# Output projection of a gated block as four pairs of block products, with weight sums made in DRAM

## The chip, the cores and the metric

The kernel runs on one core of a Trainium2 chip. The metric is the device time of one execution in microseconds, as the median of several runs. The profile is of one execution and gives the span from its first to its last instruction.

## What is computed

A hybrid block on x of shape (1, 1024, 1024), all in float32. The input is normalised and projected; an attention branch and a pooling branch give 512 channels each; each is projected to 1024 channels, gated, and the sum goes through the output projection, the residual and a last norm:

```python
a = jnp.einsum('bsc,cd->bsd', y_attn, w_branch_attn)
p = jnp.einsum('bsc,cd->bsd', y_pool, w_branch_pool)
gate_a, gate_p = jnp.split(jax.nn.sigmoid(g_merge), 2, axis=-1)
merged = gate_a * a + gate_p * p
h = h + jnp.einsum('bsd,de->bse', merged, w_out)
return rms_norm(h, norm_final)
```

## The kernel before

Every float32 product is made of three matmuls of reduced float32 parts: an operand is split into a high part (a copy on ScalarE that rounds) and a low part (a subtraction on VectorE), and hi x hi, hi x lo and lo x hi are summed in PSUM. `split` (used by `operand`, `put` and `split_tile`) is that pair of instructions. A matmul has a stationary operand of 128x128 and a moving one of up to 512 columns.

The work runs in stages, on a list of items: the input projection of the latents; fourteen `Pair` items; the up-projections of the latents; attention over eight heads, in whose gaps the eight items of the pooling branch's projection (`run_branch_p`) run; eight `BranchItem`s for the attention branch; and the output projection.

A `Pair` computes two 128-channel rows of the input projection at once. It treats the 2x2 blocks of the weights (A11 to A22, each split in four tiles) and of the input (`B`, seven block combinations b11, b21, b22, t1 to t4 that are made once) by Winograd's variant of Strassen's scheme: seven block products of 12 matmuls in place of eight, with sums S1 to S4 of the A blocks made on VectorE (`both`) and additions out of PSUM afterwards. `load` fetches w_z, `preps` lists the steps that make the operands of the next item, and `tick` runs one of them after each product.

The pooling branch's gate is fetched in halves into `go` buffers, multiplied with the product in PSUM and stored in DRAM (`mp_d`). A `BranchItem` t loads w_ba, its gate, `mp_d[t]` and one row tile of w_o, multiplies, adds, and splits the merged tile and the w_o tile into high and low parts in SBUF. The output projection then takes eight row tiles of 128 tokens, each as two halves of 512 columns over eight blocks of channels (24 matmuls for a half); the last row tile is cut in 512, 256 and 256 columns to shorten its end. Each row adds the residual, is squared and summed on ScalarE, scaled on VectorE and stored.

The order of the instructions on each engine comes from `Plan.order`, a list scheduler: it gives each operation a cost, takes the one that can start first, and among those that start within 30 ns the one that comes first in the program. Buffers come from rings of tags (`SLOTS`): 45 "t" slots of 1024 floats per partition, two each of wh, wl and go, one wr, and eight PSUM banks (s two double ones, p two, o, f). A tag's slots are handed out strictly in the order in which the program first uses the buffers. All DMAs are issued in order on SP.

Of the kernel before, what the change touches and what calls it, by code (L numbers as in the profile page):

```python
# [14 lines left out]
P = 128  # L15
# [194 lines left out]
def hybrid_block_kernel(  # L210
# [42 lines left out]
    def dram(rows, name):  # L253
        b = Buf(lambda: tc.dram_tile([rows, T], F32, name=name), None)
        return View(b, 0, rows, 0, T)
# [116 lines left out]
    def dma(o, x):  # L372
        v = o if isinstance(o, View) else x
        p0, p1, c0, c1 = v.box
        plan.add(
            "SP",
            lambda: nc.sync.dma_start(real(o), real(x)),  # L377
            450,
            views(x),
            views(o),  # L380
            (p1 - p0) * (c1 - c0) * 4,
        )
# [86 lines left out]
    mp_d = [dram(P, f"mp_d{t}") for t in range(8)]  # L469
# [411 lines left out]
    merged = [None] * 8  # L881
    wo = [None] * 8


    class Pair(Item):
# [3 lines left out]
        ORDER = (("A11", "b11"), ("S2", "t2"), ("S1", "t1"), ("S3", "t3"), ("A12", "b21"), ("A22", "t4"), ("S4", "b22"))  # L889

        def __init__(self, i, posts, beside=()):
            self.i, self.posts, self.beside = i, posts, dict(beside)
            self.turn = len(items)
            self.src = w_z[i]
# [8 lines left out]
        def operand(self, name):  # L903
            j = len(self.ops)
            t = buf(("wh", "t", "wl", "t", "wh", "t", "wl")[j], T, F32R, "wp")
            split(t[:, lft], t[:, rgt], self.q[name])
# [7 lines left out]
        def preps(self):  # L914
# [4 lines left out]
                lambda: (self.both("S1", "A21", "A22", A, "A22"), self.both("S3", "A11", "A21", S, "A21")),  # L919
                lambda: (self.both("S2", "S1", "A11", S, "A11"), self.operand("S2")),  # L920
                lambda: self.operand("S1"),
                lambda: self.operand("S3"),
                lambda: self.operand("A12"),
                lambda: (self.both("S4", "A12", "S2", S, "A12"), self.operand("S4")),
            ]

        def product(self, bank, which, first):
# [4 lines left out]
            if which in self.beside:  # L932
                self.beside[which].go(self)
            a, b = self.ORDER[which]
            for k, ((ah, al), (bh, bl)) in enumerate(zip(self.ops[a], B[b])):
# [9 lines left out]
        def run(self, it, tick):  # L945
# [17 lines left out]
            self.product(c, 2, True)  # L963
            tt(c22, c, c21, ALU.add)
            tick()
            self.product(b, 3, False)
# [3 lines left out]
            self.product(a, 4, False)  # L970
            tt(c11, a, state["r"][:, lft], ALU.mult)
            tick()
            self.product(b, 5, False)
            tt(c21, b, c21, ALU.add)
            times(c21, lft)
            self.posts[1](o2)
            tick()
            self.product(c, 6, False)
            tt(c12, c, c12, ALU.add)
            times(c12, rgt)  # L980
            self.posts[0](o1)
            tick()
# [3 lines left out]
    def step_on(n):  # L986

        for _ in range(n):
# [3 lines left out]
            pair = isinstance(it, Pair)  # L992
# [4 lines left out]
            while ready[0] < min(i + 2, len(items)):  # L997
                nxt = items[ready[0]]
                ready[0] += 1
                todo += nxt.preps() if isinstance(nxt, Pair) else [nxt.split]  # L1000
# [66 lines left out]

    items.append(KrItem(w_kr, 32, 8, run_kr))
# [27 lines left out]
    gate_pair(14, [(4, q), (6, kv)])  # L1096
    for p in range(4):
# [11 lines left out]

    def run_branch_p(t):  # L1110
        def run(it):
            mov = halves(yp)
            for h, c in enumerate((lft, rgt)):
                g = buf("go", 512, F32, "go")
                dma(g, gate_d[8 + t][:, c])
# [9 lines left out]
                tt(g, ps, g, ALU.mult)  # L1125
                dma(mp_d[t][:, c], g)
# [8 lines left out]

    class BranchItem(Item):
        def __init__(self, t):
# [3 lines left out]
        def load(self):  # L1141
            super().load()
            self.g, self.m = t32("gate"), t32("mp")
            dma(self.g, gate_d[self.t])
            dma(self.m, mp_d[self.t])

        def go(self, it):
            t, g = self.t, self.g
            raw = t32("wo")
            dma(raw, w_o[t])  # L1150
            acc = next_acc()
            prod(acc, it.h, it.l, halves(ys))
            wo[t] = (tr("woh"), tr("wol"))
            for c in (lft, rgt):
                if c is lft or t < 4:
                    split(wo[t][0][:, c], wo[t][1][:, c], raw[:, c])
                else:
                    late.append((wo[t][0][:, c], wo[t][1][:, c], raw[:, c]))
            for ps, a, b in acc.spans:
                tt(g[:, a:b], ps, g[:, a:b], ALU.mult)  # L1160
            tt(g, g, self.m, ALU.add)
            merged[t] = split_tile(g)

    late = []
    raw_tag[0] = "t"
    for t in range(8):
        items.append(BranchItem(t))

# [90 lines left out]

    for v in late:  # L1260
        split(*v)
    nf = t32("nf")
    dma(nf, nfin)
    for i in range(8):
        sl = slice(128 * i, 128 * i + 128)
        res = t32("res")
        dma(res, xr[sl, :])
        last = i == 7
        cuts = [0, 512, 768, T] if last else [0, 512, T]
        tags = "pps" if last else "pp" if i % 2 else "of"  # L1270
        ss, st = cell(3), cell()
        junk = t32("junk")
        spans = list(zip(cuts, cuts[1:]))
        for n, (a, b) in enumerate(spans):
            c = slice(a, b)
# [104 lines left out]
```

## Time and profile before

| | us |
|---|---|
| median of 3 runs | 711.28 |
| lowest, highest | 710.94, 712.90 |
| profiled execution, device time | 712.28 |
| its span | 710.2 |
| TensorE busy | 691.1 |
| VectorE busy | 524.2 |
| ScalarE busy | 319.7 |
| GpSimd busy | 104.8 |

The busy time of TensorE counts overlapping matmuls once. The share of a whole span is an average over stages; what one stage costs is read from windows of that stage. Idle time of an engine that isn't the bottleneck costs nothing by itself.

### The profile page before, as it was taken

What the parts mean: (1) busy time and instruction counts of PE and PEld (TensorE: products, weight loads), DVE (VectorE), ACT (ScalarE), POOL (GpSimd) and SP (SyncE); (2) the same over time, 40 slices, a digit from 0 to 9 for tenths busy, and PEclk for the clock granted to TensorE, in tenths of its full rate; (3) what the DMA queues carried; (4) which work ended last, traced back from release to release, by engine and by line L of the source; (5) the groups of instructions that cost most, each with busy time, mean ns of one, the idle gap of its engine ahead of it and who ended that gap; (6) DMA issues with size and microseconds to landing.
All of it is one profiled execution on the core that took longest, in us unless ns stands there. A gap on an engine that the chain in (4) does not pass through costs nothing.

```text
span 710.2 us, 9562 instructions
## 1 busy us (share of the span) xinstructions
PE 691.1 (97%) x3428; PEld 581.1 (82%) x3428; DVE 524.2 (74%) x823; ACT 319.7 (45%) x587; POOL 104.8 (15%) x140
## 2 busy tenths in 40 slices
PE   8999999999999999999998999999999999999996
PEld 6878888888878878888786799989999777888885
DVE  5688898777978689789869678887887859932223
ACT  5864424331423344333346467666666525421112
POOL 0020100300002030300101044545443100000000
PEclk9999999999999999999999999999999999999999
DMA  8957433122715436233777986554322499413131
GB/s 313 375 177 260 149 119 120 68 111 99 279 59 179 177 118 235 91 132 103 284 256 293 325 187 189 142 138 109 106 75 74 160 326 409 143 60 118 60 118 60
DMA packets 39567, 120.70 MB, mean 170 GB/s; under 512 B 5088, under 2 KB 6240, under 8 KB 39520
## 3 DMA queue, kind: packets, MB, share of 16 engines
q1 hardware_dynamic: 39520, 120.09, 49.4%
q8 instruction: 27, 0.44, 0.2%
q14 instruction: 20, 0.16, 0.1%
HBM read 81.14 MB, written 37.88 MB: 168 GB/s over the span
## 4 chain that ended last, share of the span: by engine, by line
PE 83%; DMA 6%; DVE 5%; ACT 2%; issue 2%; SPq 1%; DVEq 0%; ACTq 0%
PE ps L275 28%; PE pb L275 22%; PE po L275 12%; PE sc L275 7%; PE o L275 5%; PE pf L275 5%; PE pt L282 4%; DMA wr<-w_bp 2%; DMA wr<-w_uq 1%; DMA wo<-w_o 1%; DVE lo L308 1%; SPq L377 1%; DMA x<-xT 1%; DMA wr<-w_uv 1%; DVE ra L308 1%
## 5 line engine op out<-in xcount | busy, mean ns | idle before, releaser
L275 PE MATMUL pb<-t,wp 128*128 128x512 f32 x504 | 121.6, 390 | 0.0
L275 PE MATMUL ps<-xa,wp 128*128 128x512 f32 x392 | 113.0, 390 | 0.0
L275 PEld LDWEIGHTS pb<-t,wp 128*128 128x128 f32 x504 | 94.5, 188 | 19.8 <-DVE z L308 0.2
L298 ACT CAST wp<-wr 128x512 fp32r<-128x512 f32 x98 | 58.9, 619 | 102.2 <-DVE wr L308 38.3
L275 PEld LDWEIGHTS ps<-xa,wp 128*128 128x128 f32 x392 | 73.6, 188 | 15.2
L308 DVE TENSOR_TENSOR wp<-wr,wp 128x512 fp32r<-128x512 f32 x98 | 72.6, 756 | 8.8 <-ACT wp L298 8.8
L322 POOL TENSOR_SCALAR pr<-pr,small 128x384 f32<-128x384 f32 (+4 forms) x64 | 48.3, 759 | 72.1 <-DVE small L348 56.6
L290 ACT ACTIVATE pr<-sc,small 128x384 f32<-128x384 f32 (+4 forms) x64 | 47.7, 746 | 20.6 <-DVE small L357 19.7
L308 DVE TENSOR_TENSOR pT<-pt,pT 128x512 fp32r<-128x512 f32 (+1 forms) x80 | 48.6, 633 | 8.9 <-ACT pT L298 8.3
L357 DVE TENSOR_REDUCE small<-sc 128x1 f32<-128x128 f32 (+3 forms) x64 | 47.5, 750 | 9.2 <-PE sc L275 8.7
L308 POOL TENSOR_TENSOR z<-z,sig 128x512 f32<-128x512 f32 x16 | 23.5, 1493 | 199.7 <-ACT sig L290 197.3
L275 PE MATMUL po<-woh,hi 128*128 128x512 f32 (+1 forms) x136 | 51.3, 377 | 0.0
L275 PE MATMUL po<-woh,lo 128*128 128x512 f32 (+1 forms) x136 | 51.3, 377 | 0.0
L275 PE MATMUL po<-wol,hi 128*128 128x512 f32 (+1 forms) x136 | 51.2, 377 | 0.0
L298 ACT CAST pT<-pt 128x512 fp32r<-128x512 f32 (+1 forms) x80 | 41.2, 545 | 17.2 <-PE pt L282 16.5
L275 PE MATMUL o<-pT,v 128*128 128x256 f32 (+1 forms) x320 | 47.7, 282 | 0.6 <-DVE oa L308 0.4
L275 PEld LDWEIGHTS o<-pT,v 128*128 128x128 f32 x320 | 43.7, 189 | 3.2 <-DVE oa L308 0.8
L308 DVE TENSOR_TENSOR z<-pb,z 128x512 f32<-128x512 f32 x42 | 28.9, 689 | 23.3 <-PE pb L275 18.3
L308 DVE TENSOR_TENSOR res<-po,res 128x512 f32<-128x512 f32 (+1 forms) x17 | 11.2, 660 | 46.9 <-PE po L275 46.9
L275 PE MATMUL ps<-xb,wp 128*128 128x512 f32 x112 | 43.6, 389 | 0.0
L282 PE MATMUL pt<-ident,pr 128*128 128x128 f32 x288 | 42.1, 274 | 0.0
L275 PE MATMUL ps<-t,wp 128*128 128x512 f32 x168 | 41.1, 391 | 0.8 <-DVE z L308 0.8
(192 smaller groups left out, 1382.8 us busy)
## 6 DMA issues: line engine op xcount, KB each, us to landing
wr<-w_z SPq DMA_DIRECT2D x30, 512.0 KB, 4.9
gate_d<-z SPq DMA_DIRECT2D x16, 512.0 KB, 2.6
xt<-xr SPq DMA_DIRECT2D x8, 512.0 KB, 10.3
go<-gate_d SPq DMA_DIRECT2D x16, 256.0 KB, 2.8
mp_d<-go SPq DMA_DIRECT2D x16, 256.0 KB, 2.8
gate<-gate_d SPq DMA_DIRECT2D x8, 512.0 KB, 7.3
mp<-mp_d SPq DMA_DIRECT2D x8, 512.0 KB, 8.2
wo<-w_o SPq DMA_DIRECT2D x8, 512.0 KB, 8.7
```

Source lines behind the costliest of these rows:

```text
L275: nc.tensor.matmul(real(o), real(a), real(b), start=s, stop=e, **kw)
L282: nc.tensor.transpose(real(o), real(a), real(ident))
L290: nc.scalar.activation(real(o), real(x), func, scale=real(scale), **kw)
L298: lambda: nc.scalar.copy(real(o), real(x)),
L308: plan.add(eng, lambda: e.tensor_tensor(real(o), real(a), real(b), op), c, [a, b], [o], port=port)
L322: e.tensor_scalar(real(o), real(a), real(s1), real(s2), op0, op1)
L357: lambda: nc.vector.tensor_reduce(real(o), real(a), axis=AX.X, op=ALU.max, negate=True),
L377: lambda: nc.sync.dma_start(real(o), real(x)),
```

## The change

The output projection becomes Strassen's scheme too. The merged tiles are stored in DRAM (`m_d`, two halves of 512 channels) and read back as blocks of 128 tokens; `Ahead` makes the first product (A11 b11) of four pairs of row tiles, and four `OutPair`s make the other six. The blocks of w_out and their four sums t1 to t4 are split as moving operands while the `BranchItem`s run. The sums are made in DRAM during the `Pair` stage: a plain transfer copies one block, and a transfer issued by GpSimd adds a second, negated on ScalarE where needed; hooks (`after`) tie each transfer to a product of some `Pair`. The products of the `Pair`s come in another order, with fewer additions on VectorE and more copies on ScalarE. The pooling branch's gated rows stay in SBUF (`mp`), loaded per head during attention, and the buffers `mp_d` are gone.

```diff
+    def dma_add(o, x):
+        plan.add(
+            "POOL",
+            lambda: nc.gpsimd.dma_start(real(o), real(x), accum_op=ALU.add),
+            1200,
+            views(o, x),
+            views(o),
...
-        ORDER = (("A11", "b11"), ("S2", "t2"), ("S1", "t1"), ("S3", "t3"), ("A12", "b21"), ("A22", "t4"), ("S4", "b22"))
+        ORDER = (("A11", "b11"), ("A12", "b21"), ("S2", "t2"), ("S1", "t1"), ("S3", "t3"), ("S4", "b22"), ("A22", "t4"))
...
-            self.product(a, 0, True)
-            acopy(c21, a)
+            b = buf("p", 512, F32, "pb")
+            self.product(b, 0, True)
+            acopy(c11, b)
             tick()
-            b = buf("p", 512, F32, "pb")
-            self.product(b, 1, True)
-            tt(c12, b, c21, ALU.add)
+            self.product(a, 1, True)
+            tt(c11, a, c11, ALU.add)
+            times(c11, lft)
...
+    def take(name, src, k):
+        def f(late):
+            rows = slice(128 * k, 128 * k + 128)
+            n = buf("go", 512, F32, "neg")
+            dma(n, src[rows, :], late)
+            act(n, n, AF.Copy, scale=-1.0)
+            dma_add(wt_d[name][rows, :], n)
+        return f
...
+    hooks = {1: [copy("t1", w_top, 512), copy("t3", w_low, 512)]}
+    for k, n in enumerate((2, 3, 4, 6)):
+        hooks[n] = [take("t1", w_top[:, 0:512], k), take("t3", w_top[:, 512:T], k)]
+    hooks[7] = [copy("t2", wt_d["t3"], 0)]
+    hooks[8] = [lambda late: dma_add(wt_d["t2"], w_top[:, 0:512])]
+    hooks[10] = [copy("t4", wt_d["t2"], 0)]
+    for k in range(4):
+        hooks.setdefault(11 + k // 2, []).append(take("t4", w_low[:, 0:512], k))
...
     def run_branch_p(t):
...
-                g = buf("go", 512, F32, "go")
-                dma(g, gate_d[8 + t][:, c])
...
-                tt(g, ps, g, ALU.mult)
-                dma(mp_d[t][:, c], g)
+                tt(g[:, c], ps, g[:, c], ALU.mult)
...
     class BranchItem(Item):
...
+            for n in BLOCKS[self.t : self.t + 1]:
+                src, c = blocks_at[n]
+                for j in range(2):
+                    raw = t32("wo")
...
+            for raw in self.blocks:
+                w = tr("wo")
+                split(w[:, lft], w[:, rgt], raw)
+                W.setdefault(BLOCKS[t], []).append((w[:, lft], w[:, rgt]))
+            for n, ps in enumerate(acc.halves):
+                c = (lft, rgt)[n]
+                tt(g[:, c], ps, g[:, c], ALU.mult)
+                tt(g[:, c], mp[t][:, c], g[:, c], ALU.add)
+                dma(rows_of(t)[:, c], g[:, c])
...
+    def rows_in(o, i, half):
+        dma(
+            o.via(lambda a: a.rearrange("p (k c) -> p k c", k=4)),
+            m_d[half][:, 128 * i : 128 * i + 128].via(lambda a: a.rearrange("(k p) c -> p k c", p=P)),
+        )
...
+    class Ahead:
...
+        def run(self, it, tick):
+            tick()
+            s1, s2 = buf("s", T, F32, "ps"), buf("s", T, F32, "ps")
+            first["b"] = [buf("o", 512, F32, "pb"), buf("f", 512, F32, "pb"), s1[:, lft], s2[:, lft]]
+            first["c"] = [s1[:, rgt], s2[:, rgt], None, None]
+            for i in range(4):
+                t, bank = self.ops[i], first["b"][i]
+                for k, (bh, bl) in enumerate(W["b11"]):
+                    ah, al = t[:, 128 * k : 128 * k + 128], t[:, 512 + 128 * k : 640 + 128 * k]
+                    mms([(bank, ah, bh, k == 0, False), (bank, ah, bl, False, False), (bank, al, bh, False, k == 3)])
+                tick()
...
+    class OutPair(Pair):
+        TAGS = ("t", "wh", "wl", "t", "wh", "wl")
+        ORDER = (None, ("A12", "b21"), ("S2", "t2"), ("S1", "t1"), ("S3", "t3"), ("S4", "b22"), ("A22", "t4"))
...
+        def begin(self):
+            self.q, self.ops = {}, {}
+            raws = [t32("mr"), t32("mr")]
+            for half, e in ((1, 0), (1, 1), (0, 1), (0, 0)):
+                c = (lft, rgt)[half]
+                rows_in(raws[e][:, c], self.i + 4 * e, half)
...
+        def preps(self):
+            S, A = ALU.subtract, ALU.add
+            return [
+                self.begin,
+                lambda: (self.operand("A12"), self.operand("A22", -1.0)),
+                lambda: (self.both("S1", "A21", "A22", A, "A22"), self.both("S3", "A11", "A21", S, "A21")),
+                lambda: (self.both("S2", "S1", "A11", S, "A11"), self.operand("S2")),
+                lambda: self.operand("S1"),
+                lambda: (self.operand("S3"), self.both("S4", "A12", "S2", S, "A12"), self.operand("S4")),
+            ]
...
+            self.product(b, 6, False)
+            R.add(1, 0, b)
+            R.square(1, 0)
+            R.finish(1, i == 3)
...
+        mp[h] = t32("mp")
+        dma(mp[h], gate_d[8 + h])
...
-    for i in range(8):
-        sl = slice(128 * i, 128 * i + 128)
-        res = t32("res")
-        dma(res, xr[sl, :])
-        last = i == 7
-        cuts = [0, 512, 768, T] if last else [0, 512, T]
...
```

## Rows read from the trace of the kernel before

**Rows 1.** The page: busy time, share of the span and instructions of each engine.
```profile
PE 691.1 (97%) x3428; PEld 581.1 (82%) x3428; DVE 524.2 (74%) x823; ACT 319.7 (45%) x587; POOL 104.8 (15%) x140
```

**Rows 2.** The page: shares of the chain that ended last, by engine.
```profile
PE 83%; DMA 6%; DVE 5%; ACT 2%; issue 2%; SPq 1%; DVEq 0%; ACTq 0%
```

**Rows 3.** That chain in order of time: start us, us, what.
```profile
105.11 2.72 PE pb L275 x12
...
616.70 87.36 PE po L275 x408
```

**Rows 4.** Windows: stretch, length, each engine's busy us (instructions); TensorE clock, DMA share, GB/s.
```profile
105.10:124.20 19.10, 19.10 (x86) 15.81 (x85) 15.97 (x27) 9.13 (x14) 0.00 (x0) 1.00 0.35 133
...
566.00:616.70 50.70, 49.54 (x217) 40.33 (x216) 40.45 (x50) 19.46 (x30) 0.00 (x0) 1.00 0.81 296
616.70:704.10 87.40, 87.34 (x408) 73.11 (x407) 29.06 (x48) 16.36 (x43) 0.00 (x0) 1.00 0.26 92
704.10:710.20 6.10, 0.00 (x0) 0.00 (x0) 1.48 (x5) 1.52 (x4) 0.00 (x0) 0.86 0.23 86
```

**Rows 5.** Groups of VectorE from 566 to 616.7: busy us, mean ns, idle before.
```profile
L308 DVE TENSOR_TENSOR wol<-wo,woh 128x512 fp32r<-128x512 f32 x14 | 9.3, 685 | 0.3 <-ACT woh L298 0.3
L308 DVE TENSOR_TENSOR gate<-gate,mp 128x1024 f32<-128x1024 f32 x7 | 8.6, 1224 | 0.2
L308 DVE TENSOR_TENSOR lo<-gate,hi 128x1024 fp32r<-128x1024 f32 x6 | 7.4, 1225 | 0.8 <-ACT hi L298 0.8
...
L308 DVE TENSOR_TENSOR gate<-ps,gate 128x1024 f32<-128x1024 f32 x4 | 4.9, 1218 | 0.0
```

**Rows 6.** Groups of the whole span: busy us, mean ns, idle before.
```profile
L308 DVE TENSOR_TENSOR pT<-pt,pT 128x512 fp32r<-128x512 f32 (+1 forms) x80 | 48.6, 633 | 8.9 <-ACT pT L298 8.3
...
L308 POOL TENSOR_TENSOR z<-z,sig 128x512 f32<-128x512 f32 x16 | 23.5, 1493 | 199.7 <-ACT sig L290 197.3
...
L308 DVE TENSOR_TENSOR z<-pb,z 128x512 f32<-128x512 f32 x42 | 28.9, 689 | 23.3 <-PE pb L275 18.3
...
L298 ACT CAST woh<-wo 128x512 fp32r<-128x512 f32 x16 | 9.3, 619 | 9.1 <-DMA wo<-w_o 9.1
```

**Rows 7.** Transfers of 256 KB: stores' median landing; loads and stores of go together.
```profile
mp_d<-go SPq DMA_DIRECT2D x16, 256.0 KB, 2.8
...
DMA to landing us min/median/max: 2.0/2.8/8.8
```

**Rows 8.** DMA from 557 to 617: GB/s in 40 slices of 1.5 us; median landings.
```profile
GB/s 97 337 311 352 126 63 303 208 235 393 421 414 392 332 49 291 298 418 407 423 412 406 416 399 404 412 404 401 410 412 401 317 19 0 0 0 0 137 276 265
...
gate<-gate_d SPq DMA_DIRECT2D x8, 512.0 KB, 7.3
...
wo<-w_o SPq DMA_DIRECT2D x8, 512.0 KB, 8.7
```

**Rows 9.** Waits: who for whom, us in total, times, longest; TensorE, then SP (540 to 620).
```profile
PE ps L275 <- DVE wl L308: 1.7, 2, 1.5
...
PE pf L275 <- DVE go L308: 1.0, 1, 1.0
...
SPq L377 <- DVE go L308: 25.2, 5, 10.1
```

**Rows 10.** Timeline: start us, us, engine, what; the last branch product, then the tail.
```profile
616.51 0.69 DVE L308 TENSOR_TENSOR gate<-pb,gate 128x512 f32<-128x512 f32 x1 [0.79 <-PE pb L275]
...
704.08 0.42 DVE L308 TENSOR_TENSOR res<-po,res 128x256 f32<-128x256 f32 x1 [1.38 <-PE po L275]
704.54 0.42 ACT L290 ACTIVATE junk<-res 128x256 f32<-128x256 f32 x1 [2.36 <-DVE res L308]
...
705.80 0.72 ACT L290 ACTIVATE res<-res,small 128x512 f32<-128x512 f32 x1 [0.23 <-DVE small L348]
```

**Rows 11.** Groups of VectorE from 650 to 680: busy us, mean ns, idle before.
```profile
L308 DVE TENSOR_TENSOR res<-po,res 128x512 f32<-128x512 f32 x6 | 4.1, 692 | 20.1 <-PE po L275 20.1
L329 DVE SCALAR_TENSOR_TENSOR res<-res,small,nf 128x1024 f32<-128x1024 f32 x3 | 3.9, 1284 | 0.1
L348 DVE RECIPROCAL small<-small 128x1 f32<-128x1 f32 x3 | 0.5, 164 | 1.1 <-ACT small L290 1.1
```

More of the change, by code (lines that the diff above doesn't have):

```diff
@@ L969, in run @@
             tick()
[L970 to L978, printed above, removed]
+            self.product(c, 5, False)
             tt(c12, c, c12, ALU.add)
@@ L999, in step_on @@
                 ready[0] += 1
-                todo += nxt.preps() if isinstance(nxt, Pair) else [nxt.split]
+                todo += nxt.preps() if hasattr(nxt, "preps") else [nxt.split]
             tick = lambda: todo and todo.pop(0)()
@@ L1096, in hybrid_block_kernel @@
     gate_pair(14, [(4, q), (6, kv)])
+    for n, it in enumerate(i for i in items if isinstance(i, Pair)):
+        for j, f in enumerate(hooks.get(n, [])):
+            it.after[1 + 3 * j] = f
     for p in range(4):
@@ L1134, in hybrid_block_kernel @@
     ys = []
+    BLOCKS = ("b11", "b21", "t2", "t1", "t3", "b22", "t4")
+    blocks_at = {
+        "b11": (w_top, 0),
+        "b21": (w_low, 0),
+        "b22": (w_low, 512),
+        **{n: (wt_d[n], 0) for n in wt_d},
+    }
+    W = {}
     class BranchItem(Item):
@@ new lines, in hybrid_block_kernel, with __init__, load, preps @@
+    class OutPair(Pair):
+        TAGS = ("t", "wh", "wl", "t", "wh", "wl")
+        ORDER = (None, ("A12", "b21"), ("S2", "t2"), ("S1", "t1"), ("S3", "t3"), ("S4", "b22"), ("A22", "t4"))
+        moving = W
+        def __init__(self, i):
+            self.i, self.beside, self.after = i, {}, {}
+        def load(self):
+            pass
+        def begin(self):
[4 more added lines that the diff above has]
+                rows_in(raws[e][:, c], self.i + 4 * e, half)
+                self.q[f"A{e + 1}{half + 1}"] = raws[e][:, c]
+            self.rows = Rows(self.i)
+        def preps(self):
+            S, A = ALU.subtract, ALU.add
[7 more added lines that the diff above has]
+            ]
+        def run(self, it, tick):
+            i, R = self.i, self.rows
+            b = first["b"][i]
+            c = first["c"][i] or buf("of"[i - 2], 512, F32, "pb")
+            a = buf("p", 512, F32, "pb")
+            tick()
+            R.add(0, 0, b)
+            self.product(a, 1, True)
+            R.add(0, 0, a)
+            R.square(0, 0)
+            tick()
+            self.product(b, 2, False)
+            R.add(0, 1, b)
+            tick()
+            self.product(c, 3, True)
+            R.add(1, 1, c)
+            tick()
+            self.product(b, 4, False)
+            R.add(1, 1, b)
+            R.square(1, 1)
+            if i == 3:
+                R.scale(1, 1)
+            tick()
+            self.product(c, 5, False)
+            R.add(0, 1, c)
+            R.square(0, 1)
+            R.finish(0)
+            tick()
+            self.product(b, 6, False)
+            R.add(1, 0, b)
+            R.square(1, 0)
+            R.finish(1, i == 3)
@@ L1167, in hybrid_block_kernel @@
         items.append(BranchItem(t))
+    items.append(Ahead())
+    for i in range(4):
+        items.append(OutPair(i))
     items[0].load()
```

174 lines of the change are left out of this document (100 added, 74 removed).

## Prediction

> **What bounds the kernel now.** I read the busy line and the chain first: TensorE is busy for 691.1 of 710.2 us [rows 1], and the chain of waits lies on it for 83% [rows 2]. So a change pays by the matmuls it removes, and loses what it makes TensorE wait. Its granted clock is 1.00, the 2.4 GHz level, in every stretch with matmuls [rows 4]. The pace is read from a whole product: 12 matmuls of 512 columns take 2.72 us on the chain, 0.2267 each [rows 3]; the 0.39 us of a single record overlaps its neighbours and is not used. Then the stages, by windows. In the branch stage (566 to 616.7) TensorE has 49.5, VectorE 40.5 of 50.7 us and the DMA engines 0.81: all three are near their limit. The output stage (616.7 to 704.1) is TensorE alone: 87.3 of 87.4, VectorE 29.1. Behind the last matmul comes a tail of 6.1 us [rows 4].
>
> **The output matmuls.** Before, 8 row tiles x 2 halves x 8 blocks x 3 terms are 384 matmuls of 512 columns (one half is cut in two, so there are 408 records); 384 x 0.2267 = 87.0, which the chain confirms with 87.36 [rows 3]. After, 4 pairs x 7 products x 12 = 336, or 76.2 us. That removes 48 x 0.2267 = **10.9 us** from a stage where nothing else is late. The 48 matmuls of Ahead are the first products of the four pairs; they need only merged tiles 0 to 3 and the block b11, and last 10.9 us.
>
> **VectorE in the branch stage.** Out go the splits of w_o (14 in that stretch, 9.3 us) and of merged (6, 7.4 us) [rows 5]. In come 28 splits of the seven weight blocks at 0.685 = 19.2, four for Ahead = 2.7, and 1.6 for gate work in halves (14 x 0.685 for 8.6, 8 x 0.685 for 4.9) [rows 5]. So 40.5 - 9.3 - 7.4 + 19.2 + 2.7 + 1.6 = 47.3 of 50.7 us: it fits, with 3.4 us to spare. SP issues the loads in order, and in before it once stood 10.1 us behind VectorE's go products; TensorE lost 1.0 by these [rows 9]. Those loads and stores go away, since the gates of the pooling branch now stay in SBUF: up to 1.0 gained, I take 0.5. The stage moves more bytes: 7.3 MB of blocks, 6.3 of gates and w_ba, 4.2 written to m_d and 2.1 read back, 19.9 MB; at the 400 GB/s and more of its full slices [rows 8] that is 50 us, just the stage. I take no loss before the last branch item, and keep 3 us for the range.
>
> **The start of Ahead.** Two of its banks are o and f, which the last branch item also fills; before, the product out of that bank ran 0.69 us just behind the matmuls [rows 10]. Its operand tiles come from the 45 "t" slots: 28 weight tiles, 8 of ys, 2 of the last item and 3 of Ahead's loads leave exactly four, so the last of them wait until item 6 has stored its rows or the ys fall free. I take 1.5 us; from 0 (an s bank is free and its operand there) to 5 (operand splits and the old bank queue up behind VectorE).
>
> **Merged rows through DRAM.** This is the new wait. From the last branch matmul: 0.2 us, then two VectorE operations of 0.685 for each half, so the halves leave after 1.6 and 2.9 us. A 256 KB store landed in 2.8 us, and so did the loads of that size (the median covers both) [rows 7]. With 0.3 for the issue, A12 is there at 1.6 + 2.8 + 0.3 + 2.8 = 7.5 and split at 9.0 (0.62 on ScalarE [rows 6], 0.69 on VectorE); Ahead ends at 1.5 + 10.9 = 12.4, so product 1 doesn't wait. A22 is there at 8.8; its split, S1, S3, S2 and the split of S2 are 1.3 + 3 x 0.69 + 1.3 = 4.7, ready at 13.5, needed at 12.4 + 2.72 = 15.1. So Ahead hides the round trip with 1.6 us to spare; from there each further us is lost one for one. The reads are of 512-byte pieces, which no row shows: from 2.0 to 8.8, the shortest and the longest landing of a 256 KB transfer here [rows 7]; I take 2.8, its median.
>
> **VectorE in the output stage.** A pair has 6 operand splits, 4 sums and 7 additions out of PSUM, 17 x 0.69 = 11.7, and two rows of 1.28 + 0.16 + 0.16 [rows 11], 3.2: 14.9 us in the 16.3 of its 72 matmuls, 91%. In the pair stage VectorE has 15.97 of 19.10, 84%, and TensorE no gap [rows 4], so this is tighter than anything shown. The first pair must also make the second's operands: 14.9 + 10 x 0.69 = 21.8 us, between A12 at 7.5 and the pair's end at 12.4 + 16.3 = 28.7, which are 21.2. I take 1.5 us for operands that come late, from 0 to 5.
>
> **The tail.** The last product is 512 columns wide instead of 256: 0.69 for 0.42 in the addition [rows 10, 11], 0.63 for 0.42 in the square (0.62 for 512 columns in a ScalarE copy [rows 6]); the scaling is 0.72 on ScalarE either way [rows 10]. **+0.5 us.**
>
> **Pairs, weight sums, attention.** A regrouped pair has 4 instead of 6 additions out of PSUM on VectorE, 1.4 us less at 0.689 [rows 6], and two more copies on ScalarE, about 1.2 more beside 9.1 of 19.1 [rows 4]. TensorE has the same 84 matmuls, so nothing is won. The sums are 28 more issues on SP, 12 negations of 0.62 on ScalarE and 13 adding transfers on GpSimd, spread over 13 pairs of 19 us. An adding transfer has no row; GpSimd sits idle for 199.7 us before its silu products alone [rows 6], and the next reader of a sum follows one to two pairs later. No wait goes away here, so it can't gain; the worst is SP standing behind a sum with w_z behind it, which is fetched two items ahead, and the 10.1 us of before cost 1.0 [rows 9]. I take 0, from 0 to 2. In attention the eight mp tiles leave pT 4 slots instead of 12 in the last head; the 80 pT cost VectorE 48.6 us [rows 6] of a stage three times as long, so two in use are the rule. I take 0, up to 2.
>
> **Sum.** -10.9 + 1.5 + 1.5 + 0.5 - 0.5 = -7.9 us. On the span of 710.2 that gives 702.3. The profiled run took 712.28, 2.1 above its span, and the median is 711.28; taken off the median, 703.4. Nearly all unknown terms can only add, so I put **704**.
>
> **Rivals.**
> - All waits hidden: -10.9 + 0.5 - 0.5 = -10.9, 700.4. For it: 1.6 us of slack in the round trip, VectorE below 100% in each stage. Against: bank o must be emptied first. 0.15.
> - VectorE sets the pace, at the upper ends for Ahead and the first pair: -10.9 + 5 + 5 + 0.5 = -0.4, 710.9. For it: 47.3 of 50.7 and 21.8 of 21.2. Against: 84% without a gap in the pair stage. 0.14, anywhere from 707 to 713.
> - Slower: the round trip in a loaded queue. While the queue was full, w_o landed in 8.7 us and the gates in 7.3 [rows 8]. If the store to m_d and the read each take 8.7, A22 comes at 2.9 + 8.7 + 0.3 + 8.7 = 20.6 and S2 at 25.3, against 15.1: 10.2 us of waiting, -7.9 + 10.2 = +2.3, 713.6. It decides from 7.9 us of waiting on, when both landings together pass 5.6 + 1.6 + 7.9 = 15.1 us. Against: in before the queue had fallen to 0 GB/s some 10 us ahead of that point [rows 8]. 0.08.
> - Slower still, by the clock: in the tail, where TensorE stood idle for 6.1 us, the granted clock was 0.86, and it was 1.00 wherever its waits were short, 1.5 us and less behind VectorE [rows 4, 9]. If a wait of some 6 us falls into the round trip and the clock drops to its lower level, the next two products take 2 x 2.72 more: -7.9 + 6 + 5.4 = +3.5, 714.8. 0.05. The Trainium skill (TensorE: Matmul & The Clock Gate, "HAM oscillation — how this bites in real kernels") holds that a gap long enough between bursts of matmuls throttles the array, so that the next burst starts cold. The drop in the tail fits that, but no matmul follows it, so no run here shows a cold restart.
>
> **How the numbers follow.** The forecast, from 702 to 707, has 0.58. Some 0.03 lie below 699.5 (short waits of before vanish as well) and 0.13 above 713, so the range is 699.5 to 713. A measurement of this kernel can tell 0.3% (2.1 us: 709.1 and 713.4) from no change. Faster: 0.58 + 0.15 + 0.04 of VectorE's case = 0.77; within: its other 0.10; slower: 0.08 + 0.05 = 0.13.
>
> **What will show it.** In the profile after: TensorE's busy time down by about 11 us, and 336 matmuls in the output stage at 0.2267; a gap of 1 to 2 us ahead of Ahead, ended by gate products or operand splits; no transfer of merged rows that ends a wait of TensorE; VectorE above 90% from 570 to 640 and small gaps in the first pair; a tail of 6.6 us; pair and attention stages as long as before. Wrong would be: a wait on a read of m_d behind Ahead (the round trip), a granted clock below 1.00 after it, waits of TensorE for w_z in the pair stage (SP behind a sum), or waits for pT in the last heads.

## The result, and the profile after

The changed kernel took 705.67 us (median of four runs, 704.76 to 706.78) against 712.09 (710.94 to 713.4) for the kernel before on the same chip: ratio 0.9899, 95% interval 0.9869 to 0.9929. The prediction was 704.0, between 699.5 and 713, faster. The profiled run took 705.3 us, its span 703.4; before it was 712.28 and 710.2.

Time and sign came out as forecast, but not by the steps forecast: that the time is so near is in part luck, as the table below shows. First the page's busy line after (it answers to [rows 1]) and its line of granted clocks in 40 slices:

```profile
PE 681.5 (97%) x3356; PEld 573.3 (82%) x3356; DVE 539.8 (77%) x863; ACT 355.8 (51%) x657; POOL 115.6 (16%) x153
...
PEclk9999999999999999999999989999999999999999
```

TensorE is busy 9.6 us less, not 10.9, and one slice, the 24th (404 to 422 us), shows a clock below nine tenths. That slice lies in attention, where the change touches only the pooling branch's gates: they are loaded per head into `mp` and multiplied in place, and the loads into `go` and the stores to `mp_d` are gone.

To split the span, take marks that both kernels share: the first product of the squares (`zsq`), the first score product (`sc`), the last branch matmul (taken as the start of the first output matmul behind it), the last output matmul and the end. The first two are the starts of these groups of TensorE (tile view: count, min/median/max ns of one, from when to when), before and then after:

```profile
L275 PE MATMUL pb<-ones,zsq x32: 164/250/251, 61.8 to 78.9; 128*128 128x1 f32 x32
L275 PE MATMUL sc<-kh,qh x96: 220/368/479, 401.2 to 547.4; 128*128 128x384 f32 x24, 128*128 128x512 f32 x24, 128*128 128x320 f32 x16, 128*128 128x448 f32 x16
```

```profile
L275 PE MATMUL pb<-ones,zsq x32: 164/250/250, 60.4 to 77.5; 128*128 128x1 f32 x32
L275 PE MATMUL sc<-kh,qh x96: 220/389/481, 396.0 to 550.8; 128*128 128x384 f32 x24, 128*128 128x512 f32 x24, 128*128 128x320 f32 x16, 128*128 128x448 f32 x16
```

The first output matmul, in the timelines of before and of after:

```profile
616.53 0.39 PE L275 MATMUL po<-woh,hi 128*128 128x512 f32 x1
```

```profile
618.11 1.52 PE L275 MATMUL ps<-wo,wm 128*128 128x512 f32 x6
```

The last marks are read from the windows of after (stretch, length, busy us of PE, PEld, DVE, ACT, POOL, then clock, DMA share, GB/s), which answer to [rows 4]:

```profile
618.10:695.70 77.60, 76.91 (x337) 62.72 (x335) 55.51 (x94) 27.59 (x62) 0.00 (x0) 1.00 0.47 153
695.70:703.40 7.70, 0.00 (x0) 0.00 (x0) 2.52 (x5) 1.74 (x4) 0.00 (x0) 0.83 0.36 136
```

| stretch | before us | after us | difference | forecast |
|---|---|---|---|---|
| start to the first squares | 61.8 | 60.4 | -1.4 | 0 |
| squares to the first score (pairs, weight sums) | 339.4 | 335.6 | -3.8 | 0 |
| first score to the last branch matmul | 215.3 | 222.1 | +6.8 | -0.5 |
| output matmuls | 87.6 | 77.6 | -10.0 | -7.9 |
| behind the last matmul | 6.1 | 7.7 | +1.6 | +0.5 |
| span | 710.2 | 703.4 | -6.8 | -7.9 |

The first line is spread from one execution to the next: in two of the kernels below that differ in the merged rows alone (early `mp` 0, another layout) the mark lies at 63.0 and at 60.6, and in those two, shown in this order, the granted clock differs near the start:

```profile
8.00:12.00 4.00, 4.00 (x12) 3.19 (x11) 2.68 (x4) 2.97 (x5) 0.00 (x0) 0.58 1.05 405
```

```profile
8.00:12.00 4.00, 4.00 (x19) 3.25 (x19) 2.50 (x4) 3.31 (x5) 0.00 (x0) 1.00 1.03 399
```

The second and third lines, -3.8 and +6.8, are what the prediction took at about zero. They nearly cancel, and with them the rest nearly gives the total.

**Where the 6.8 us came from.** The chain of waits of after (start, us, what) shows one transfer of 10.6 us:

```profile
396.98 7.09 DMA kl<-kr_d
...
404.09 10.63 DMA mp<-gate_d
```

And the timeline with the idle time before each, in brackets:

```profile
414.74 0.69 DVE L308 TENSOR_TENSOR mp<-pf,mp 128x512 f32<-128x512 f32 x1 [5.30 <-DMA mp<-gate_d]
415.49 0.80 PE L275 MATMUL pf<-hi,wh 128*128 128x512 f32 x1 [4.87 <-DVE mp L308]
```

The gates of the first head, `mp` 0, are loaded behind all loads of the second head, in a stretch where the DMA engines are nearly full (share 1.02 from 396 to 404 us, 0.96 from 404 to 412). VectorE's queue stands 5.30 us at the gate product, whose operand isn't there, and TensorE stands 4.87 us for a bank. Then it runs at a lower clock (windows of after, clock third from the end):

```profile
412.00:416.00 4.00, 0.51 (x1) 0.50 (x2) 1.26 (x2) 0.00 (x0) 0.00 (x0) 0.76 0.93 222
416.00:420.00 4.00, 4.00 (x16) 3.52 (x15) 1.54 (x5) 1.35 (x3) 1.71 (x2) 0.50 0.37 79
420.00:424.00 4.00, 4.00 (x25) 3.53 (x25) 1.92 (x6) 1.86 (x6) 0.37 (x1) 0.89 0.01 2
```

0.50 is the 1.2 GHz level, for at least 4 us; half of those 4 and a tenth of the next 4 are lost, some 2.4 us. 4.87 + 2.4 = 7.3 us, a little more than the stretch lost; the first experiment below shows that the load's place cost more than the 6.8, and that the rest of the stretch became shorter.

**What made 3.8 us.** Waits of before that have no counterpart after (TensorE from 62 to 396 us: who for whom, us in total, times, longest); the one for `zkv` lies just behind the last pair, at 351.15 us, the others among the pairs:

```profile
PE ps L275 <- DVE z L308: 0.8, 1, 0.8
PE pb L275 <- DVE zkv L308: 0.6, 1, 0.6
PE pb L275 <- DVE lo L308: 0.5, 1, 0.5
PE pb L275 <- ACT hi L298: 0.3, 1, 0.3
```

In windows, TensorE's idle time from the squares to the first score fell from 5.2 to 2.8 us, and VectorE's busy time from 279.7 to 262.5. So 2.4 of the 3.8 are seen as idle time. Each gap also costs about 0.16 us more than it shows, because a matmul's record lasts 0.389 us while the next can start after 0.2267; with five gaps gone (the four listed and one of 0.1) that is an estimated 0.8. The last 0.6 I could not place.

**The output stage.** It needs 336 matmuls at 0.2267, 76.2 us; it took 77.6. One wait of TensorE in it shows in the list, 0.61 us, behind the round trip. Chain of after from the last store of a merged row to that wait, and TensorE's timeline around it:

```profile
620.96 4.50 DMA m_d<-gate
...
625.53 3.52 DMA mr<-m_d
...
632.61 0.61 DVE wp L308
```

```profile
628.99 2.88 PE L275 MATMUL pb<-wo,wp 128*128 128x512 f32 x12
631.93 0.73 PE L275 MATMUL ps<-wo,wp 128*128 128x512 f32 x2
633.27 1.20 PE L275 MATMUL ps<-wo,wp 128*128 128x512 f32 x4 [0.61 <-DVE wp L308]
```

`Ahead` starts at 618.11 and the product behind it at 628.99, 10.88 us later, which is 48 matmuls without a gap. The product with S2 starts 2.94 us behind that where a product takes 2.72, and its low part comes 1.34 us behind its first matmul where two matmuls take 0.45: about 1.1 us lost by the starts, of which 0.61 shows as idle time.

### The profile page after: what moved, and what is told of

Its sections match the earlier page's. It is cut to its first block, busy times and chain, and to the rows that moved or that the text cites. A ratio compares the mean times of both kernels' runs of the same rounds, so it can differ in the third digit from the quotient of the medians.

```text
span 703.4 us, 9678 instructions
## 1 busy us (share of the span) xinstructions
PE 681.5 (97%) x3356; PEld 573.3 (82%) x3356; DVE 539.8 (77%) x863; ACT 355.8 (51%) x657; POOL 115.6 (16%) x153
## 4 chain that ended last, share of the span: by engine, by line
PE 84%; DMA 6%; DVE 5%; ACT 2%; issue 1%; SPq 1%; DVEq 0%; ACTq 0%
PE pb L275 33%; PE ps L275 30%; PE sc L275 6%; PE pf L275 6%; PE o L275 4%; PE pt L282 4%; DMA mp<-gate_d 2%; DMA m_d<-gate 1%; DMA kl<-kr_d 1%; DVE lo L308 1%; DMA wr<-w_uv 1%; DVE ra L308 1%; DVE gate L308 1%; SPq L378 1%; DMA wr<-w_bp 1%
## 5 line engine op out<-in xcount | busy, mean ns | idle before, releaser
L275 PE MATMUL ps<-xa,wp 128*128 128x512 f32 x224 | 74.0, 390 | 0.0
L275 PEld LDWEIGHTS ps<-xa,wp 128*128 128x128 f32 x224 | 42.0, 188 | 8.7
L275 PE MATMUL pb<-xa,wp 128*128 128x512 f32 x168 | 40.7, 389 | 0.0
L275 PE MATMUL pb<-wo,wp 128*128 128x512 f32 x168 | 39.9, 389 | 0.0
L275 PE MATMUL sc<-kh,qh 128*128 128x384 f32 (+4 forms) x96 | 36.2, 377 | 2.3 <-ACT pr L290 2.3
L275 PEld LDWEIGHTS pb<-wo,wp 128*128 128x128 f32 x168 | 31.5, 188 | 6.6
L275 PEld LDWEIGHTS pb<-xa,wp 128*128 128x128 f32 x168 | 31.5, 188 | 6.5
L275 PEld LDWEIGHTS ps<-t,wp 128*128 128x128 f32 x168 | 31.4, 188 | 6.5
```

The lines of the kernel that those rows point to most:

```text
L275: nc.tensor.matmul(real(o), real(a), real(b), start=s, stop=e, **kw)
```

## Experiments: the two terms that were not forecast

**mp 0 loaded earlier.**

```diff
-    step_on(n_pre)
+    step_on(n_pre - 8)
+    load_mp(0)
+    step_on(8)
...
-        mp[h] = t32("mp")
-        dma(mp[h], gate_d[8 + h])
+        if h:
+            load_mp(h)
```

> The changed kernel with one load moved: the gate of the first pooling item (mp 0) is fetched before the value products instead of behind the loads of the second head, 13 transfers earlier on SP; nothing else is edited. Theory A, the load is what cost the time: in the changed kernel TensorE waits 4.9 us at 410.6 for the product out of bank f, which waits on VectorE for mp 0 (landed in 10.6 us), and the granted clock is 0.50 from 416 to 420. Then the wait and the low clock go, the stretch from the first score matmul to the last branch matmul shrinks from 222.1 us to 215 to 216, and the time falls by 6 to 7.5 us, to 698 to 700. Rival B, the queue is full there whatever comes first (DMA share 1.0 from 380 to 412): the loads of the second head land about 1.3 us later, TensorE waits for them instead, and the time stays within 703 to 706.

698.45 us (698.28 to 701.0), ratio to the kernel before 0.9808, interval 0.9772 to 0.9844, clear of the change's own 0.9869 to 0.9929. The wait for `mp` is 0.8 us where it was longest 4.9, and the clock stays at its 2.4 GHz level where it was 0.50:

```profile
416.00:420.00 4.00, 4.00 (x26) 3.62 (x27) 2.91 (x7) 1.97 (x5) 0.73 (x1) 1.00 0.97 226
```

Theory A holds. The stretch from the first score to the last branch matmul takes 213.4 us, 8.7 less than in the change and 1.9 less than before; the output matmuls take 79.3 us there, 1.7 more, with waits of 0.7 and 0.5 us for `wp`. So the place of one load cost 0.9% of the kernel, about as much as the whole change brought (1.0%).

**The gates in SBUF, alone, in the kernel before.** Only the rows of `mp_d` and `go` go away and the `mp` loads per head come in.

```diff
-                g = buf("go", 512, F32, "go")
-                dma(g, gate_d[8 + t][:, c])
...
-                tt(g, ps, g, ALU.mult)
-                dma(mp_d[t][:, c], g)
+                tt(g[:, c], ps, g[:, c], ALU.mult)
...
+        mp[h] = t32("mp")
+        dma(mp[h], gate_d[8 + h])
```

> The kernel before with only the pooling branch's gates moved into SBUF: mp loaded per head, multiplied in place, no go loads and no stores to mp_d; the output projection is the old one. Theory A: the same wait appears at the start of attention (4 to 6 us behind mp 0, then the lower clock), and the time is 4 to 7 us above the kernel before, 716 to 719. Rival C, the wait is an accident of the new order of the whole program and not of this part: no wait on mp above 1 us, and the time is that of before or up to 1 us less, 710.5 to 712.5.

719.25 us (717.47 to 721.03), ratio 1.0091 (1.0057 to 1.0125): slower by 6.5 us. TensorE's largest wait in this kernel:

```profile
PE pf L275 <- DVE mp L308: 5.4, 3, 4.1
```

The granted clock falls behind it here too, to 0.58 from 420 to 424 us. So this part alone brings a loss, and theory A holds. The ratios give 0.9899 - 0.9808 = 0.0091 for moving one load in the change and 0.0091 for adding the part to the kernel before; with intervals of some 0.003 each way, and since the two edits are not the same, the equal digits are chance. In the profiled run, 5.4 us longer than before, 4.7 lie between the first score and the last branch matmul; 1.6 lie ahead of it, where TensorE waits 1.7 us for `z` in a pair, far from any `mp`. Whether the part causes that wait too isn't shown.

**The regrouped pairs alone, and the change without them.** The first puts the new order of the pairs' products and preparations into the kernel before; the second puts the old order into the changed kernel.

```diff
-        ORDER = (("A11", "b11"), ("S2", "t2"), ("S1", "t1"), ("S3", "t3"), ("A12", "b21"), ("A22", "t4"), ("S4", "b22"))
+        ORDER = (("A11", "b11"), ("A12", "b21"), ("S2", "t2"), ("S1", "t1"), ("S3", "t3"), ("S4", "b22"), ("A22", "t4"))
...
```

> The kernel before with only the regrouped pairs (their order of products, of operand steps and of additions). Attention begins at 396.0 in the changed kernel and at 401.2 in the one before, a gain that was not forecast. Theory P, the regrouping gave it, by 1.4 us less VectorE work in each pair: attention begins 3 to 5 us earlier and the time is 707 to 709. Rival Q, short waits around the pairs come and go with any change of order: attention begins within 1.5 us of 401 and the time is 711 to 713.

> The changed kernel with the old pairs put back (their order of products, of operand steps and of additions); the weight sums stay tied to products of the same numbers. Theory P: the 5.2 us ahead of attention come back, attention begins near 400 and the time is 709 to 711. Rival Q: attention begins at 396 to 397.5 and the time is 704.5 to 707.

Alone: 708.07 us (704.55 to 710.98), ratio 0.9936 (0.9909 to 0.9962). The change without them: 710.05 (708.22 to 711.6), ratio 0.9967 (0.9946 to 0.9988). The two marks, first of the pairs alone, then of the change with the old pairs:

```profile
L275 PE MATMUL pb<-ones,zsq x32: 164/250/250, 61.1 to 78.2; 128*128 128x1 f32 x32
L275 PE MATMUL sc<-kh,qh x96: 220/368/481, 396.9 to 542.9; 128*128 128x384 f32 x24, 128*128 128x512 f32 x24, 128*128 128x320 f32 x16, 128*128 128x448 f32 x16
```

```profile
L275 PE MATMUL pb<-ones,zsq x32: 164/250/250, 62.8 to 79.9; 128*128 128x1 f32 x32
L275 PE MATMUL sc<-kh,qh x96: 220/389/481, 403.0 to 554.4; 128*128 128x384 f32 x24, 128*128 128x512 f32 x24, 128*128 128x320 f32 x16, 128*128 128x448 f32 x16
```

From mark to mark: 335.8 and 340.2 us. Over all kernels the old pairs give 339.4, 341.0 (gates alone) and 340.2, the new ones 335.6, 335.8 (early `mp` 0) and 335.8, whatever else is changed. The regrouping is worth about 4.5 us, shown from both sides (theory P's times); which of its edits does it, the fewer additions on VectorE or the other order of operands and products, was not tried apart. The weight sums, which only half of these kernels have, cost nothing that this can see.

## Experiments: the cover, the queue and the tail

All of these start from the kernel with the early `mp` 0, so that the other loss is out of the way; the tail in halves and the residual rows ahead of the stores keep the other layout too.

**No cover.** `Ahead`, the 48 first products, goes in front of the last branch item.

```diff
     for t in range(8):
+        if t == 7:
+            items.append(Ahead())
         items.append(BranchItem(t))
-    items.append(Ahead())
...
-            acc = next_acc()
+            acc = Acc("pp") if t == 7 else next_acc()
```

> The kernel with the early load of mp 0 (e1), with the item that needs no merged row of the last branch (12 products of the output stage, started ahead) moved from behind the last branch item to in front of it, so that no TensorE work stands between the last gate and the first sums of the merged rows. The work is the same. Theory C (the cover is worth what the round trip takes): after the last branch item TensorE waits about 9 us (last gate 1, store 4.5, read 3.5, split and sum 1.2, less what the queue holds), the granted clock falls in the stretch behind the wait, as it did behind the wait of 4.9 us for mp 0 in the kernel after, which adds 2 to 4 us, and the time is 708 to 713 us. Rival (a round trip of two landings of 2.8 us, as the prediction sized it, and no loss of clock): a wait of 6 to 7 us and 704.5 to 706 us. Rival N (the round trip is hidden by the queue of other work anyway): under 702 us.

712.73 us (708.52 to 718.79), ratio 0.9999 (0.9962 to 1.0035): about 14 us lost, the whole gain of the version it starts from. TensorE's longest waits, and windows where they fall:

```profile
PE pb L275 <- ACT wp L298: 6.9, 1, 6.9
PE pb L275 <- ACT wm L298: 3.2, 1, 3.2
```

```profile
612.00:618.00 6.00, 3.56 (x8) 2.77 (x9) 3.58 (x6) 2.98 (x5) 0.00 (x0) 0.65 0.62 243
618.00:624.00 6.00, 6.00 (x22) 4.83 (x21) 4.07 (x8) 2.39 (x4) 0.00 (x0) 0.78 0.22 77
...
636.00:642.00 6.00, 1.16 (x3) 0.93 (x4) 1.18 (x2) 0.77 (x2) 0.00 (x0) 0.64 0.73 228
642.00:648.00 6.00, 5.97 (x22) 4.49 (x21) 5.39 (x9) 3.29 (x6) 0.00 (x0) 0.79 1.08 339
```

The wait behind the last branch item is 6.9 us, the 6 to 7 of the rival and not the 9 of theory C, since the last stores here met an empty queue and landed in 2.0 us and the read in 2.9. The rival had no loss of clock, and that is where it fails: each of the two waits is followed by a stretch at a lower clock. The time falls into C's range, but partly by the 3.2 us and their lower clock, which C did not have. The experiment is not pure: moving `Ahead` also brought its need for its own rows too early (the 3.2 us), so the 14 us are the price of having no cover for either round trip. The profiled run is the slowest of ten (718.79), and its clock also falls in attention, behind waits of at most 1.4 us:

```profile
420.00:424.00 4.00, 4.00 (x20) 3.61 (x19) 1.49 (x4) 1.57 (x5) 0.74 (x1) 0.67 0.88 177
```

**Residual rows behind the reads.** The residual's two 512 KB transfers of each pair are issued behind the pair's reads of `m_d`.

```diff
-                dma(self.t[e], xr[128 * self.row[e] : 128 * self.row[e] + 128, :])
+                dma(self.t[e], xr[128 * self.row[e] : 128 * self.row[e] + 128, :], late)
...
+            self.rows = Rows(self.i, self.q["A22"])
...
-            self.rows = Rows(self.i)
...
```

> The kernel with the early load of mp 0 (e1), with the residual rows of each output pair (2 transfers of 512 KB) issued after the pair's reads of the merged rows instead of before them. In e1 the stores of the last branch item leave at 616.1 us, 4.9 us behind these 2 transfers, and take 4.8 us to land, the reads 3 to 4, and TensorE waits twice in the first pair behind the operands, 0.7 and 0.5 us. Theory Q (the store and the reads are slow because the residual's 1 MB is in the queue with them): the last stores land in 2.8 to 3.3 us, the two waits go, and the time falls by 1.0 to 1.2 us, to about 697.4. Rival F (the form of the stores and reads, or the landing in DRAM itself, is what takes 4.8 and 3.5 us): both durations and both waits stay within 0.5 us of e1 and the time stays at 698.4. Rival V (the residual arrives late): VectorE's queue stands behind res in the first pair and the time rises by 1 to 3 us.

700.96 us (700.64 to 702.33), ratio 0.9842 (0.9806 to 0.9878): no gain. The round trip itself got shorter: from the end of the last gate operation to VectorE's first operation on the merged rows it takes 8.55 us with the early `mp` 0 and 4.54 here. The waits for `wp` are gone, and others came in their place, one each in the second, third and fourth pair (at 644.5, 662.2 and 680.0 us):

```profile
PE ps L275 <- DVE res L308: 2.3, 2, 1.2
...
PE pb L275 <- DVE res L308: 1.3, 1, 1.3
```

So theory Q holds for the transfer, and the median goes the way of V (the intervals overlap), though not by a late residual: VectorE stood 3.4 to 3.9 us at additions whose product wasn't done yet. That the order of its queue moved with the loads is the likely reason; it isn't shown.

**Another layout of the merged rows.** Stores of 512-byte pieces and reads of one contiguous 256 KB, where it was the other way round.

```diff
-    m_d = [dram(512, f"m_d{i}") for i in range(2)]
+    m_d = [dram(T, f"m_d{i}", 512) for i in range(2)]
...
-            m_d[half][:, 128 * i : 128 * i + 128].via(lambda a: a.rearrange("(k p) c -> p k c", p=P)),
+        dma(o, m_d[half][128 * i : 128 * i + 128, :])
```

> The kernel with the early load of mp 0 (e1), with the merged rows laid out in DRAM by column block (8 blocks of 128 rows by 4 times 128 columns), so that each read takes one contiguous run of 256 KB, of 2 KB to a partition, and each store writes pieces of 512 bytes; in the kernel after it is the other way round, stores of 2 KB to a partition and reads of pieces of 512 bytes. Theory S (the size of the pieces sets the landing): the reads fall from a median of 4.4 us to 3 or less, the stores rise from 4.2 to 5 or more, and since the last store and the first read follow one another the time changes by less than 1 us, 697.5 to 699.4. Theory L (what else is in the queues sets it): both medians stay within 0.5 us of 4.4 and 4.2, and the time stays within 0.5 us of 698.4.

697.76 us (696.6 to 698.43), ratio 0.9789 (0.9759 to 0.9819), not to be told from the 0.9808 it starts from. Median landings, of the early `mp` 0 and then of this one:

```profile
m_d<-gate SPq DMA_DIRECT2D x16, 256.0 KB, 5.9
mr<-m_d SPq DMA_DIRECT2D x16, 256.0 KB, 4.8
```

```profile
m_d<-gate SPq DMA_DIRECT2D x16, 256.0 KB, 5.5
mr<-m_d SPq DMA_DIRECT2D x16, 256.0 KB, 4.5
```

Both go down by 0.3 to 0.4, where theory S wanted them to part. The expectation had put down the medians of the changed kernel, 4.2 and 4.4, for those of the version it starts from; against the right ones, L holds: no effect of the size of the pieces is seen.

**Residual rows ahead of the stores.** With that layout and the tail below, the first pair's residual is fetched before the rows of branch item 6 are stored.

```diff
             dma(nf, nfin)
+            first["rows"] = Rows(0)
...
-            self.rows = Rows(self.i)
+            self.rows = first["rows"] if self.i == 0 else Rows(self.i)
```

> The same kernel (e9) with the residual rows of the first output pair (2 transfers of 512 KB) issued ahead of the stores of branch item 6 instead of between those and the stores of the last item. Theory Q (the 1 MB in the queue ahead of the last stores sets their landing of 4.5 to 5.8 us): the last stores land in 2.0 to 3.0 us, as the one store did that met an empty queue in the run without cover (2.0), the first sums of the merged rows start about 2 us earlier than in e8, and TensorE has no wait in the first pair; the time falls by at most 0.5 us, since e8 had hardly a wait left there. Rival: the transfers now delay the stores of items 4 to 6 and with them the rows taken ahead, and TensorE waits behind wm: 698 to 700.

697.85 us (696.52 to 700.43), ratio 0.979 (0.9772 to 0.9808). From the last gate operation to the first operation on merged rows, in its timeline:

```profile
617.42 0.69 DVE L308 TENSOR_TENSOR gate<-mp,gate 128x512 f32<-128x512 f32 x1
...
622.67 0.69 DVE L308 TENSOR_TENSOR wp<-mr,wp 128x512 fp32r<-128x512 f32 x1 [2.79 <-ACT wp L298]
```

That is 622.67 - 618.11 = 4.56 us. In six versions with the residual's 1 MB between the stores it is 6.7 to 9.0 (7.4 in the change itself, 7.5 in the version this one starts from); in the two that issue it elsewhere 4.5 and 4.6. The last two stores land in 2.3 and 2.4 us. So theory Q is right on the cause: the queue, at 4.0 and 2.9 us in the two pairs of versions that differ by it. TensorE now waits 0.8 us on `wm`, the rows taken ahead, as the rival said; time isn't won, because hardly any wait was left here.

**The tail.** First the scaling of the row finished before the last went to ScalarE, then it was cut in two on VectorE.

```diff
...
-            R.finish(0)
+            if i == 3:
+                R.scale(0, 0)
+                R.scale(0, 1)
+            R.finish(0, i == 3, i == 3)
```

> The kernel with the early load of mp 0 (e1), with one more edit: of the last output pair the row that is finished before the last one is multiplied by the weight in two halves on VectorE beforehand and scaled by one 1024-wide instruction on ScalarE, so that VectorE's queue holds no scaling in front of the last addition. In e1 the last matmul ends at 691.45 us, the last addition starts 0.78 us later behind a scaling of 1.28 us that began at 691.03, and the span ends at 699.2, so that the tail is 7.75 us. Theory (the queue in front of the last addition cost the unforecast 0.8 us of the tail): the addition starts within 0.1 us of the last matmul's end, the tail is 6.9 to 7.1, and the time falls by 0.7 us, to about 697.7 us, ratio to the kernel before about 0.980. Rival (the row's scaling only changes engine): ScalarE's 1024-wide scaling of about 1.05 us stands in front of the last square, the tail stays at 7.6 to 8.0 and the time at 698.4 us.

699.74 us (698.85 to 703.78), ratio 0.983 (0.9789 to 0.987): no gain. Its timeline:

```profile
693.61 0.69 DVE L308 TENSOR_TENSOR res<-ps,res 128x512 f32<-128x512 f32 x1 [0.41 <-PE ps L275]
...
695.02 1.13 ACT L290 ACTIVATE res<-res,small 128x1024 f32<-128x1024 f32 x1
...
696.06 0.28 ACT L290 ACTIVATE small<-small,eps 128x1 f32<-128x1 f32 x1
```

The addition starts 0.04 us behind the last matmul, as the theory said, and the tail is 7.9 us all the same: the 1.13 us of scaling now stand on ScalarE in front of the last root. The rival was right, with the root in place of the square.

```diff
...
             R.square(1, 0)
+            if i == 3:
+                R.finish_rest(0)
             R.finish(1, i == 3)
```

> The kernel of the run before with the merged rows laid out by column block (e8), with one more edit: in the last output pair the scaling of the row finished before the last one is done in two halves on VectorE, one in front of the last addition (about 0.72 us in place of 1.28) and one behind it, in the gap of 0.85 us in which VectorE waits for ScalarE's square. In e8 the last matmul stands 0.74 us short of the addition behind the 1.28 us scaling. Theory (the scaling in front of the addition is what the tail lost): the addition starts 0.25 to 0.35 us behind the last matmul's end, nothing else moves, the tail falls by 0.4 to 0.5 us to about 7.25, and the time is 697.3. Rival (as the version with ScalarE showed, the half behind the addition delays the last root or the last store): tail 7.6 to 7.8 and 697.8.

Cut in two, 698.24 us (697.33 to 699.51), ratio 0.9798 (0.9781 to 0.9816). Its timeline; the last matmul ends at 688.51, the span at 695.7:

```profile
688.09 0.75 DVE L329 SCALAR_TENSOR_TENSOR res<-res,small,nf 128x512 f32<-128x512 f32 x1
688.76 0.68 DVE L308 TENSOR_TENSOR res<-ps,res 128x512 f32<-128x512 f32 x1
```

The addition starts 0.25 us late and the tail is 7.2 us, 7.7 in the version it starts from (the other layout): the theory's 0.4 to 0.5. The time doesn't resolve half a microsecond, so this is shown by the trace alone.

Three versions (another layout, tail in halves, early residual) lie at 0.979 to 0.980, each interval wholly below that of the change. I can't rank them.

## Why the prediction was right, and where not

- **The output matmuls: right.** 336 matmuls at 0.2267 us, 76.2 us, as its steps said, and the stage came out 1.4 us above that. The output projection alone was not run; if the parts add, the ratios leave 0.9899 + 0.0064 (pairs) - 0.0091 (gates) = 0.9872 for it, some 9 us.
- **The start of Ahead: mis-sized, 1.5 us for none.** TensorE has no wait there. `Ahead` takes the s bank first and the o and f banks behind it, and gets through its 48 matmuls without a gap. The prediction had this case (a free s bank) as the lower end of its range.
- **Operands late in the first pair: wrong, 1.5 us for none of its own.** The one wait there is the round trip's, below. The forecast had VectorE at 21.8 us in the 21.2 from A12 to the pair's end; it was busy for 14.92 of them (625.6 to 646.8). The second pair's operands need not all be made by the first pair's end: some are split after 647 us, and no wait follows. Also the sign that it named, above 90% from 570 to 640, did not come: 58.17 of 70 us, 83%. VectorE is as full as forecast only in the branch stage (29.89 of 31.70 us from 575 to 606.7, 94%), and there it keeps up.

```profile
570.00:640.00 70.00, 69.33 (x305) 56.75 (x305) 58.17 (x92) 26.54 (x47) 0.00 (x0) 1.00 0.89 299
625.60:646.80 21.20, 20.53 (x90) 16.37 (x89) 14.92 (x24) 8.51 (x17) 0.00 (x0) 1.00 0.72 223
```

- **Merged rows through DRAM: right on the mechanism, the landing mis-sized.** It gave 2.8 us to each of store and read by the median of [rows 7]; they took 4.50 and 3.52. S2 was ready 15.1 us behind the last branch matmul (633.22 - 618.11) instead of 13.5. TensorE, which had no wait ahead of `Ahead`, came for it at 60 x 0.2267 = 13.6 instead of 15.1, so 1.5 of the 1.6 us of spare were the wait that didn't come, and S2, 1.6 late, cost about 1.1 us. The median of [rows 7] was taken over the whole span; the store and the read here met a queue with the residual's 1 MB in it, which the prediction didn't count there.
- **Pairs: "no wait goes away here, so it can't gain" was wrong.** One window of 19.1 us without a gap [rows 4] was taken for 13 pairs. The list of waits over the whole span had 0.8, 0.5 and 0.3 us behind VectorE and ScalarE among the pairs and 0.6 just behind them. The regrouping cleared them: -3.8 us, about 4.5 in the experiments. The weight sums at 0 were right, and this is what they cost elsewhere (GpSimd's group: busy us, mean ns, idle before; then SP's wait):

```profile
L391 POOL DMA_DIRECT2D wt_d<-neg x12 | 10.6, 887 | 134.0 <-ACT neg L290 97.7 <-DMA d_d<-win 26.3 <-DMA wr<-w_z 9.9
```

```profile
SPq L378 <- DMA wt_d<-neg: 8.1, 3, 5.7
```

- **Attention: "0, up to 2" was wrong, +6.8.** By the early `mp` 0 the load's place cost 8.7 us of the stretch, and the rest of it gained 1.9, where 0.5 was forecast for the `go` transfers. The step looked at what the `mp` tiles take (slots) and not at where their loads stand: in SP's order, behind the second head, in a stretch with the DMA engines nearly full, and with VectorE's queue waiting at the first of them. The bound of 2 us was that of pT's slots, another cost altogether.
- **The clock rival: right on the mechanism, at another place.** It wanted a wait of some 6 us in the round trip; the wait was 4.87 us at `mp` 0, and the clock went to 0.50 behind it. The prediction held that no run showed a cold restart. Now one does, and it agrees with the Trainium skill (TensorE: Matmul & The Clock Gate, "HAM oscillation — how this bites in real kernels"): the burst behind a long gap starts cold. It isn't the only way here: without cover the clock was 0.67 from 420 to 424 us with no wait above 1.4 us ahead of it.
- **The queue rival** (both landings at 8.7): not here. Together the landings rose by 2.4 us over the forecast, a fifth of the way to it.
- **The tail: mis-sized, +0.5 for +1.6.** The products were ordered so that the other row's scaling, 1.28 us, stands on VectorE when the last matmul ends: 0.8 us more, of which the tail in halves gave back about 0.5. The last 0.3 are not placed.

Two terms that were not seen, -3.8 and +6.8, and others that were too careful on one side or short on the other: the total was nearer than its parts, and that is luck. With `mp` 0 where it should be, the change is worth about 14 us, below the range forecast.

## What to carry to other kernels

A stage is free of waits only if the list of waits over the whole stage says so; one window is not enough. When data is kept on chip instead of stored and reloaded, its first load still stands somewhere: look what is ahead of it in that queue, and which engine's in-order queue stops at its first reader. A wait of TensorE can be paid a second time in the clock: the five longest in these kernels (3.2 to 6.9 us) each had a stretch below full clock behind them, and once a group of shorter ones had too.

## What the runs showed of the hardware

- Behind an idle time of 4.87 us the granted clock was 0.50 for at least 4 us and 0.89 in the 4 us after; behind 3.2 us (without cover) it was 0.78 from 618 to 624 us, behind 6.9 us 0.79 from 642 to 648. Short waits went either way: with the early `mp` 0, and none above 1 us there, the clock was 1.00 from 416 to 424 us; without cover, which has that load too, it was 0.91 and 0.67 in the two halves of that stretch, with waits of up to 1.4 us ahead.
- The last two 256 KB stores landed in 2.0 to 2.1 us in an empty queue (no cover), and in 3.9 to 6.5 us behind 1 MB of loads (six versions).
- An adding transfer of 256 KB took GpSimd 0.89 us to issue and landed in 4.3 us (median of 12), the same as the plain loads of its operands at 4.3.
